# A list scheduler that plans PSUM tiles as exclusive and lets a tile pass one other in its ring

## The chip, the cores and the metric

The kernel runs on one core of one Trainium2 chip. Time is device microseconds of one execution, the median of 3 runs. The engines are TensorE (PE in the profile, with its weight loads as PEld), VectorE (DVE), ScalarE (ACT), GpSimd (POOL) and SyncE (SP), which here issues every DMA.

## The reference

Two layers of a sequence mixer over 2048 tokens of width 1024. Each layer normalises and modulates `x`, projects it once, runs two groups of four heads on the projection, joins them, projects back and adds the result to `x` with a gate.

```python
h = rms_norm(x, norm_g[l]) * (1.0 + scale[:, None]) + shift[:, None]
proj = h @ w_in[l]
gq, gk, gv, glr, gz, dq, dk, dv, dz = split_columns(proj)
...
o_gla = gla_branch(...)     # chunked linear attention: conv, forget gate, state scan, rms_norm, silu gate
o_diff = diff_branch(...)   # two softmax maps per head, p0 - lam * p1, chunk-causal; rms_norm, silu gate
y = jnp.concatenate([o_gla, o_diff], axis=-1).astype(x.dtype) @ w_out[l]
x = x + gate[:, None] * y
```

## The kernel before, in words

The 2048 tokens are cut into four units of 512. A dense product is made of three matmuls on 32-bit operands split in a high and a low half (`mm3`, `proj_T`): 128 by 128 weights against 512 columns, into one of the four PSUM tiles tagged `acc`. Each PSUM tile is 128 partitions by 512 values of 4 bytes. A second ring of four, tagged `tp`, holds the transposes (`tp`), the attention scores (`sc`) and the attention outputs (`po`).

Attention runs per layer, unit and head, 32 heads in all. `head_evac` reads a head's four `acc` tiles: per tile ScalarE copies q and k to `rw`, makes `th`, and copies v to `Vt`, and VectorE makes the gate `z` from `th` and the tile. In `qk_gen`, TensorE then transposes `rw` into two `tp` tiles. From the Q tile, ScalarE writes `qh` twice for each of two maps and VectorE writes `ql` (from the tile and `qh`) and copies it over to the other partitions; from the K tile, ScalarE writes half of `Kt` and VectorE the other half. `attn_gen` multiplies Q by K into `sc` tiles, which VectorE moves to `s` with a running minimum; ScalarE takes the exponential; TensorE transposes `s` (`tp<-ident,s`), ScalarE copies that to `aT`, and TensorE multiplies it by V into `po`.

The order of the work is not the order of that code. Python generators call a recorder (`Program.record`), which notes each instruction, the earlier ones it must follow, and the buffers it uses. `Program.order` then replays the record as a list scheduler with a table of costs and of latencies from engine to engine: it takes the engine that can start soonest, and the instruction of the lowest turn on it. `best_order` does that 60 more times with turns moved ahead of waits of TensorE, and keeps the order with the lowest planned end. `issue` emits that order; below it, a framework sets the semaphores that every instruction waits for, from the emitted order and the tiles touched.

Two rules of the planner matter here. An instruction follows earlier ones where one of the two writes what the other touches; for a PSUM tile any access is to the whole of it, but two readers are not ordered. And the tiles of one tag are given slots strictly in the order of the record (`nxt`): a tile whose predecessor has no slot yet must wait, even if a slot is free.

Of the kernel before, what the change touches and what calls it, by code (L numbers as in the profile page):

```python
# [35 lines left out]
class Buf:  # L36
    def __init__(self, pool, shape, dt, tag, name, bufs):
        self.pool, self.shape, self.dt, self.tag, self.name, self.bufs = pool, tuple(shape), dt, tag, name, bufs
        self.psum = pool.psum
        self.tile = None  # L40
# [80 lines left out]
class Program:  # L121
# [6 lines left out]

    def __init__(self, **engines):
        self.ops = []  # L130
        self.hist = {}
        self.group = {}
        self.engines = engines
# [10 lines left out]
    def record(self, e, method, args, kw):  # L144
        i = len(self.ops)
        views = [v for v in list(args) + list(kw.values()) if isinstance(v, View)]
        out = kw["out"] if "out" in kw else args[0]
        deps = set()
        for v in views:
            wr = v is out or v is kw.get("accum_out")  # L150
            h = self.hist.setdefault(v.buf, [])
            keep = []
            for j, w2, box in h:
                hit = all(a < d and c < b for (a, b), (c, d) in zip(box, v.box))
                if hit and (wr or w2) and j != i:
                    deps.add(j)
                if not (wr and all(c <= a and b <= d for (a, b), (c, d) in zip(box, v.box))):
                    keep.append((j, w2, box))
            keep.append((i, wr, v.box))
            self.hist[v.buf] = keep  # L160
        self.ops.append((e, method, args, kw, deps, self.cost(e, method, args, kw, out), {v.buf: 0 for v in views}))

    def together(self, first):

# [46 lines left out]
    def best_order(self, rounds=60):  # L211


        ops, rnd = self.ops, random.Random(0)
        turn = [float(i) for i in range(len(ops))]
        made = self.order(turn)
        best = self.span
        for _ in range(rounds):
            res, begin, end, ready = made
            lines = {e: [i for i in res if ops[i][0] == e] for e in "TAV"}  # L220
            place = {i: k for q in lines.values() for k, i in enumerate(q)}
            waits = [(begin[i] - end[j], i) for j, i in zip(lines["T"], lines["T"][1:]) if begin[i] - end[j] > 150]
            turn2 = list(turn)
            for wait, i in waits:
                if rnd.random() >= wait / 1500 * rnd.random():
                    continue
                first = begin[i] - 15000
                for _ in range(12):
                    e = ops[i][0]
                    i = max(ops[i][4], key=lambda j: end[j] + self.LAT[ops[j][0]][e], default=None)  # L230
                    if i is None or end[i] < first:
                        break
                    if (ops[i][0] in "AV" or ops[i][0] == "T" and i not in self.group) and begin[i] - ready[i] > 80:
                        q, k = lines[ops[i][0]], place[i] - 1
                        while k >= 0 and begin[q[k]] >= ready[i]:
                            turn2[i] = min(turn2[i], turn[q[k]] - 0.5)
                            k -= 1
            made2 = self.order(turn2)
            if self.span <= best:
                best, made, turn = self.span, made2, turn2  # L240
        self.span = best
        return made[0]

    def order(self, turn_of):
        ops, N = self.ops, len(self.ops)
        begin, finish = [0.0] * N, [0.0] * N
        left, uses, turn = {}, [], {}
        for o in ops:
            for b in o[6]:
# [2 lines left out]
                    turn.setdefault((b.pool, b.tag), []).append(b)  # L252
                left[b] += 1
        place = {b: k for q in turn.values() for k, b in enumerate(q)}
        nxt = dict.fromkeys(turn, 0)
        slots = {t: [{} for _ in range(q[0].bufs or q[0].pool.bufs)] for t, q in turn.items()}
        blocked = {t: [] for t in turn}
        slot, used = {}, {}
# [5 lines left out]
        ready = [0.0] * N  # L264
        free = dict.fromkeys(self.engines, 0.0)
        dma = 0.0
        pend = {e: [] for e in free}
# [4 lines left out]
        res, burst, mode = [], 0, 0  # L272
        while len(res) < N:
            while todo:
                now, todo = sorted(todo), []
                for i in now:
                    e, bufs = ops[i][0], ops[i][6]
                    new = {}
                    for b in sorted((b for b in bufs if b not in slot), key=place.get):
                        t = (b.pool, b.tag)  # L280
                        if place[b] != nxt[t] + new.get(t, 0) or len(slots[t]) <= new.get(t, 0):
                            blocked[t].append(i)
                            break
                        new[t] = new.get(t, 0) + 1
                    else:
                        for b in sorted(bufs, key=place.get):
                            if b not in slot:
                                t = (b.pool, b.tag)
                                slot[b] = min(slots[t], key=lambda u: max(u.values(), default=0.0))
                                slots[t].remove(slot[b])  # L290
                                used[b] = {}
                                nxt[t] += 1
                                todo += blocked[t]
                                blocked[t] = []
                            for e2, x in slot[b].items():
                                ready[i] = max(ready[i], x + (self.LAT[e2][e] if e != e2 or e == "S" else 0))
                        heapq.heappush(pend[e], (ready[i], turn_of[i], i))
            t, e = min((free[e] if avail[e] else max(free[e], pend[e][0][0]), e)
                       for e in free if avail[e] or pend[e])
            while pend[e] and pend[e][0][0] <= t:  # L300
                heapq.heappush(avail[e], heapq.heappop(pend[e])[1:])
            rest = [x for x in avail[e] if self.group.get(x[1]) == burst] if e == "T" and burst else ()
            if rest:
                i = min(rest)[1]
                avail[e].remove(min(rest))
                heapq.heapify(avail[e])
            else:
                i = heapq.heappop(avail[e])[1]
            if e == "T":
                burst = self.group.get(i, 0)  # L310
            if e == "S":
                dma = end = max(dma, t + 1150, flight[-8] + 2000) + ops[i][5]
                free[e] = max(t + 475, dma - 8000)
                flight.append(end)
            elif e == "A" and self.table(ops[i]) not in (None, table):
                table = self.table(ops[i])
                free[e] = end = t + ops[i][5] + 1283
            elif e == "T":
                if self.mode(ops[i]) != mode:
                    mode = self.mode(ops[i])  # L320
                    t += 160 if mode else 190
                w = int(t / win)
                warm = work.get(w - 1, 0.0) > 0.5 * win
                free[e] = end = t + ops[i][5] * (1 if warm else 2)
                if ops[i][1] == "transpose" or ops[i][2][2].shape[-1] > 1:
                    for v in range(w, int(end / win) + 1):
                        work[v] = work.get(v, 0.0) + min(end, (v + 1) * win) - max(t, v * win)
            else:
                free[e] = end = t + ops[i][5]
            res.append(i)  # L330
            begin[i], finish[i] = t, end
            for j in succ[i]:
                ready[j] = max(ready[j], end + self.LAT[e][ops[j][0]])
                nd[j] -= 1
                if nd[j] == 0:
                    todo.append(j)
            for b in ops[i][6]:
                used[b][e] = max(used[b].get(e, 0.0), end)
                left[b] -= 1
                if left[b] == 0:  # L340
                    t_ = (b.pool, b.tag)
                    slots[t_].append(used[b])
                    todo += blocked[t_]
                    blocked[t_] = []
        self.span = max(free.values()) / 1e3
        return res, begin, finish, ready

    def issue(self):
        real = lambda v: v.real() if isinstance(v, View) else v
# [978 lines left out]
```

## Time and profile before

| | us |
|---|---|
| median of 3 runs (2516.93 to 2519.32) | 2519.05 |
| the profiled execution | 2520.62 |
| its span | 2518.9 |
| TensorE busy in it | 2465.0 |
| VectorE busy | 1736.4 |
| ScalarE busy | 1285.0 |

A matmul's end in the profile is modelled: a 128 by 512 matmul shows about 0.40 us, while the next one starts about 0.23 us after it. Busy times are unions, so TensorE counts as busy for the last 0.16 us or so in which the pipeline drains. Idle time of TensorE is therefore a little less than what it lost. All recorded instructions carry one line, L355 (`issue`), so groups are told apart by tile names.

### The profile page before, as it was taken

The page shows a single profiled execution, that of the slowest core. Times are in us where ns is not written, and L with a number is a line of the kernel's source. Part 1 is how long each engine was busy: PE and PEld are TensorE (multiplying, and loading weights), DVE is VectorE, ACT ScalarE, POOL GpSimd, SP SyncE. Part 2 cuts the span into 40 slices and gives each one's busy share as a digit, 9 for nine tenths or more (in the row PEclk, how much of TensorE's full clock was granted, in tenths as well). Part 3 has the DMA queues.
Part 4 walks back from the last instruction along what each step waited for, and adds up shares of the span by engine and source line. Part 5 has one row for each costly group of instructions (what it writes and reads, how often), then busy time and mean ns, then how long its engine had stood idle before and what let it go on. Part 6 is the DMA issues. An engine that isn't in the chain of part 4 may idle for free.

```text
span 2518.9 us, 40492 instructions
## 1 busy us (share of the span) xinstructions
PE 2465.0 (98%) x13923; PEld 2025.2 (80%) x13923; DVE 1736.4 (69%) x5313; ACT 1285.0 (51%) x2760; POOL 136.2 (5%) x424
## 2 busy tenths in 40 slices
PE   8999999999999999999999999999999999999999
PEld 5787777887888888888688777888788888888887
DVE  4879767772777737677874884667636777286874
ACT  5656534562445534455763563445614556154552
POOL 0001000000000000000000010000000000000000
PEclk9999999999999999999999999999999999999999
DMA  8667876456453555444357767454474443734343
GB/s 266 251 233 281 286 247 208 156 191 211 163 186 105 189 186 172 141 136 163 109 204 267 265 247 254 169 187 153 161 251 153 142 162 119 262 102 147 130 147 126
DMA packets 204685, 474.00 MB, mean 188 GB/s; under 512 B 20736, under 2 KB 82368, under 8 KB 204480
## 3 DMA queue, kind: packets, MB, share of 16 engines
q1 hardware_dynamic: 204480, 471.41, 54.5%
q8 instruction: 111, 1.82, 0.3%
q14 instruction: 94, 0.77, 0.1%
HBM read 360.19 MB, written 111.15 MB: 187 GB/s over the span
## 4 chain that ended last, share of the span: by engine, by line
PE 79%; DVE 11%; ACT 5%; DMA 3%; issue 2%; POOL 0%; SPq 0%; POOLq 0%; ACTq 0%; DVEq 0%
PE acc L355 51%; PE sc L355 12%; PE po L355 9%; PE tp L355 7%; DVE s L355 3%; ACT qh L355 2%; DVE t L355 1%; DVE ql L355 1%; ACT s L355 1%; DMA wr<-in_w_ada_dram 1%; DVE w L355 1%; ACT t L355 1%; DVE am L355 1%; DMA Kj<-kd 1%; DVE r L355 0%
## 5 line engine op out<-in xcount | busy, mean ns | idle before, releaser
L355 PE MATMUL acc<-w,hhi 128*128 128x512 f32 x2560 | 840.5, 402 | 2.9 <-ACT w L355 1.4
L355 PEld LDWEIGHTS acc<-w,hhi 128*128 128x128 f32 x2560 | 463.7, 189 | 92.3 <-issue 4.8
L355 PE MATMUL acc<-w,hlo 128*128 128x512 f32 x1280 | 504.9, 394 | 0.0
L355 ACT ACTIVATE s<-s,mx 128x512 f32<-128x512 f32 (+15 forms) x256 | 308.2, 1204 | 291.4 <-DVE s L355 290.1
L355 PE MATMUL acc<-hhi,w 128*128 128x512 f32 x1024 | 360.0, 400 | 0.0
L355 PE MATMUL acc<-w,oh 128*128 128x512 f32 x1024 | 332.5, 398 | 2.7 <-DVE t L355 1.1
L355 DVE TENSOR_SCALAR_CACHE_REDUCE s<-sc,mx 64x64 f32<-64x64 f32 (+5 forms) x640 | 307.9, 485 | 33.0 <-PE sc L355 14.3
L355 PEld LDWEIGHTS acc<-w,hlo 128*128 128x128 f32 x1280 | 240.8, 188 | 49.0 <-issue 0.6
L355 PEld LDWEIGHTS acc<-w,oh 128*128 128x128 f32 x1024 | 189.6, 188 | 41.3 <-DVE t L355 2.6
L355 PEld LDWEIGHTS acc<-hhi,w 128*128 128x128 f32 x1024 | 192.0, 188 | 36.7 <-DVE w L355 0.4
L355 ACT COPY aT<-tp 128x512 f32<-128x512 f32 (+2 forms) x320 | 163.0, 523 | 88.2 <-PE tp L355 85.4
L355 PE MATMUL po<-Vj,aT 128*128 128x128 f32 x1536 | 204.4, 277 | 0.7 <-ACT aT L355 0.5
L355 PE MATMUL acc<-w,ol 128*128 128x512 f32 x512 | 201.5, 397 | 0.0
L355 PE MATMUL acc<-hlo,w 128*128 128x512 f32 x512 | 201.0, 393 | 0.0
L355 DVE SCALAR_TENSOR_TENSOR s<-s,r 128x512 f32<-128x512 f32 (+3 forms) x320 | 197.8, 667 | 3.0
L355 PEld LDWEIGHTS po<-Vj,aT 128*128 128x128 f32 x1536 | 190.4, 192 | 10.5 <-ACT aT L355 4.7
L355 DVE TENSOR_SCALAR_CACHE_REDUCE s<-sc 128x512 f32<-128x512 f32 (+4 forms) x256 | 158.2, 621 | 38.7 <-PE sc L355 34.5
L355 PE MATMUL tp<-ident,s 128*128 128x128 f32 x1088 | 172.9, 275 | 11.8 <-DVE ql L355 4.2
L355 PEld LDWEIGHTS tp<-ident,s 128*128 128x128 f32 x1088 | 131.9, 141 | 49.5 <-issue 12.8
L355 ACT COPY rw<-acc 128x256 f32<-128x256 f32 x128 | 48.1, 376 | 239.6 <-PE acc L355 239.6
L355 PE MATMUL sc<-Kj,qh 128*128 128x512 f32 x384 | 158.5, 413 | 3.3 <-DVE s L355 1.4
L355 ACT ACTIVATE qh<-tp,G 64x512 fp32r<-64x512 f32 x128 | 87.6, 684 | 137.1 <-PE tp L355 115.0
(183 smaller groups left out, 3682.8 us busy)
## 6 DMA issues: line engine op xcount, KB each, us to landing
w<-wd SPq DMA_DIRECT2D x424, 512.0 KB, 4.2
wd<-w SPq DMA_DIRECT2D x144, 512.0 KB, 3.7
raw<-in_w_in_dram SPq DMA_DIRECT2D x120, 256.0 KB, 5.0
Kj<-kd SPq DMA_DIRECT2D x48, 512.0 KB, 5.8
wr<-in_w_ada_dram SPq DMA_DIRECT2D x128, 128.0 KB, 3.2
kd<-Kt SPq DMA_DIRECT2D x24, 512.0 KB, 4.0
Vj<-vd SPq DMA_DIRECT2D x48, 256.0 KB, 5.4
wr<-in_w_ada_dram SPq DMA_DIRECT2D x8, 1024.0 KB, 7.4
```

Source lines behind the costliest of these rows:

```text
L355: getattr(self.engines[e], method)(*[real(a) for a in args], **{k: real(v) for k, v in kw.items()})
```

## The change

Three edits in `Program`. First, each instruction notes the PSUM buffers that it touches (`banks`), and `order` keeps, for every such buffer, the last instruction of each engine on it: one that touches the buffer from another engine starts only when these have ended, readers too. An instruction that is held goes back to its engine's queue with a new ready time (inside a group kept together, it waits in place). Second, `best_order` follows such holds as it follows dependences when it looks for what made TensorE wait. Third, `nxt` becomes `left_out`, the list of tiles without a slot: the first of it may take a free slot, and the second may pass it if another slot stays free. No arithmetic, tile or DMA is added or removed.

```diff
@@ record
         self.ops.append((e, method, args, kw, deps, self.cost(e, method, args, kw, out), {v.buf: 0 for v in views}))
+        self.banks.append({v.buf: 0 for v in views if v.buf.psum})
@@ best_order
-                    i = max(ops[i][4], key=lambda j: end[j] + self.LAT[ops[j][0]][e], default=None)
+                    i = max(ops[i][4] | {held.get(i, i)} - {i}, key=lambda j: end[j] + self.LAT[ops[j][0]][e], default=None)
@@ order
-        nxt = dict.fromkeys(turn, 0)
+        left_out = {t: list(q) for t, q in turn.items()}
...
-                        if place[b] != nxt[t] + new.get(t, 0) or len(slots[t]) <= new.get(t, 0):
+                        ahead = left_out[t].index(b, 0, 2) if b in left_out[t][:2] else N
+                        if len(slots[t]) <= ahead or new.get(t, 0) and ahead != new[t]:
                             blocked[t].append(i)
                             break
...
-                                nxt[t] += 1
+                                left_out[t].remove(b)
...
+            prior = [j for b in self.banks[i] for e2, j in bank.setdefault(b, {}).items() if e2 != e]
+            if prior:
+                last = max(prior, key=lambda j: finish[j] + self.LAT[ops[j][0]][e])
+                hold = finish[last] + self.LAT[ops[last][0]][e]
+                if hold > t:
+                    held[i], ready[i] = last, hold
+                    if not rest:
+                        heapq.heappush(pend[e], (hold, turn_of[i], i))
+                        continue
+                    t = hold
+            for b in self.banks[i]:
+                bank[b][e] = i
```

What that moves is seen in the emitted order. The first place is ScalarE in layer 0, unit 2, fourth head, from the copy ahead of its Q tile to behind its K tile. Names in brackets are the semaphores that the instruction waits for, one for each engine and several for DMA queues. Before:

```order
L355 COPY aT<-tp 128x512 [waits PE_49,Activation_49]
L355 ACTIVATE qh<-tp,G_614 64x512 [waits PE_49]
L355 ACTIVATE qh<-tp,G_614 64x512
L355 ACTIVATE qh<-tp,G_614 64x512 [waits DVE_49]
L355 ACTIVATE qh<-tp,G_614 64x512
L355 CAST Kt<-tp 64x512 [waits DMAHW6_49,DMAHW0_49,PE_49]
L355 CAST Kt<-tp 64x512
```

and after, at the same head:

```order
L370 COPY aT<-tp 128x512 [waits PE_49,Activation_49]
L370 ACTIVATE qh<-tp,G_630 64x512 [waits PE_49]
L370 ACTIVATE qh<-tp,G_630 64x512 x3
L370 CAST Kt<-tp 64x512 [waits DMAHW3_49,DMAHW0_49,PE_49]
L370 CAST Kt<-tp 64x512
```

The wait for VectorE between the second and the third `qh` is gone. It stands in 27 of the 32 heads before and in one after.

The second place is TensorE in the same head, from the PV matmuls behind the transposes of `rw` (Q and K) to the next transposes of `s`, which need a free `tp` slot. The waits are left out here. Before:

```order
L355 MATMUL po<-Vj,aT 128x128 x4
L355 MATMUL acc<-w,hhi 128x512 x2
L355 MATMUL acc<-w,hlo 128x512
L355 MATMUL acc<-w,hhi 128x512 x2
L355 MATMUL acc<-w,hlo 128x512
L355 MATMUL acc<-w,hhi 128x512 x2
L355 MATMUL acc<-w,hlo 128x512
L355 MATMUL tp<-ident,s 128x128 x4
```

and after:

```order
L370 MATMUL acc<-w,hlo 128x512
L370 MATMUL acc<-w,hhi 128x512 x2
L370 MATMUL acc<-w,hlo 128x512
L370 MATMUL acc<-w,hhi 128x512 x2
L370 MATMUL acc<-w,hlo 128x512
L370 MATMUL acc<-w,hhi 128x512 x2
L370 MATMUL acc<-w,hlo 128x512
L370 MATMUL acc<-w,hhi 128x512 x2
L370 MATMUL acc<-w,hlo 128x512
L370 MATMUL acc<-w,hhi 128x512 x2
L370 MATMUL acc<-w,hlo 128x512
L370 MATMUL tp<-ident,s 128x128 x4
```

Nine dense matmuls stood between them, and sixteen do now.

The third place is TensorE in layer 1, unit 0, second head: from the transposes of K to the first scores that read `Kt`. Before:

```order
L355 MATMUL tp<-ident,rw 128x128 x4
L355 MATMUL acc<-w,oh 128x512 x2
L355 MATMUL acc<-w,ol 128x512
L355 MATMUL acc<-w,oh 128x512 x2
L355 MATMUL acc<-w,ol 128x512
L355 MATMUL acc<-w,oh 128x512 x2
L355 MATMUL acc<-w,ol 128x512
L355 MATMUL acc<-w,oh 128x512 x2
L355 MATMUL sc<-Kt,qh 128x128
```

and after, the rows just ahead of the same matmul:

```order
L370 MATMUL acc<-w,oh 128x512 x2
L370 MATMUL acc<-w,ol 128x512
L370 MATMUL acc<-w,oh 128x512 x2
L370 MATMUL acc<-w,ol 128x512
L370 MATMUL acc<-w,oh 128x512 x2
L370 MATMUL acc<-w,ol 128x512
L370 MATMUL acc<-w,oh 128x512 x2
L370 MATMUL acc<-w,ol 128x512
L370 MATMUL acc<-w,oh 128x512 x2
L370 MATMUL acc<-w,ol 128x512
L370 MATMUL acc<-w,oh 128x512
L370 MATMUL sc<-Kt,qh 128x128
```

Eleven dense matmuls stood between the transposes and the scores; now there are nineteen, so that the transposes are no longer among the twelve rows.

## Rows read from the trace of the kernel before

**Rows 1.** The page's part 1: busy time of each engine, share, instructions.

```profile
PE 2465.0 (98%) x13923; PEld 2025.2 (80%) x13923; DVE 1736.4 (69%) x5313; ACT 1285.0 (51%) x2760; POOL 136.2 (5%) x424
```

**Rows 2.** Busy times by stretch: the first 63 us.

```profile
core 0: us, PE busy (x) PEld busy (x) DVE busy (x) ACT busy (x) POOL busy (x), PEclk, DMA share, GB/s
0.00:63.00 63.00, 51.51 (x320) 33.27 (x320) 31.24 (x111) 34.24 (x70) 4.27 (x16) 1.00 0.87 266
```

**Rows 3.** Waits of PE: who for whom, us in total, times, longest.

```profile
PE sc L355 <- DVE Kt L355: 7.4, 11, 1.1
...
PE tp L355 <- DVE ql L355: 4.2, 4, 1.1
PE tp L355 <- DVE s L355: 4.0, 7, 1.5
PE tp L355 <- DVE z L355: 3.1, 6, 1.5
PE po L355 <- ACT aT L355: 2.6, 5, 1.0
PE sc L355 <- DVE s L355: 2.4, 6, 0.6
...
PE tp L355 <- ACT aT L355: 1.8, 2, 0.9
...
PE acc L355 <- DVE z L355: 0.4, 1, 0.4
```

**Rows 4.** Waits of DVE and ACT between accesses to one PSUM tile.

```profile
DVE z L355 <- ACT Vt L355: 116.7, 52, 18.4
...
DVE ql L355 <- ACT qh L355: 80.3, 50, 4.7
...
ACT qh L355 <- DVE ql L355: 21.2, 26, 1.6
```

**Rows 5.** Timeline, layer 0, unit 2, fourth head: start, length, engine, tiles, idle.

```profile
826.36 1.38 ACT L355 ACTIVATE qh<-tp,G 64x512 fp32r<-64x512 f32 x2 [0.59 <-PE tp L355]
...
827.77 0.74 DVE L355 SCALAR_TENSOR_TENSOR ql<-tp,G,qh 64x512 fp32r<-64x512 f32 x1 [1.64 <-PE po L355]
...
828.54 1.38 ACT L355 ACTIVATE qh<-tp,G 64x512 fp32r<-64x512 f32 x2 [0.81 <-DVE ql L355]
...
829.42 0.39 PE L355 MATMUL acc<-w,hlo 128*128 128x512 f32 x1
...
829.96 0.76 DVE L355 SCALAR_TENSOR_TENSOR ql<-tp,G,qh 64x512 fp32r<-64x512 f32 x1 [0.99 <-ACT qh L355]
...
830.86 0.63 PE L355 MATMUL tp<-ident,s 128*128 128x128 f32 x4 [1.05 <-DVE ql L355]
```

**Rows 6.** Timeline, layer 1, unit 0, second head.

```profile
1312.82 0.60 PE L355 MATMUL tp<-ident,rw 128*128 128x128 f32 x4
...
1313.96 0.62 PE L355 MATMUL acc<-w,oh 128*128 128x512 f32 x2
1314.42 0.39 PE L355 MATMUL acc<-w,ol 128*128 128x512 f32 x1
...
1315.33 0.61 PE L355 MATMUL acc<-w,oh 128*128 128x512 f32 x2
1315.59 0.42 DVE L355 CAST ql<-ql 64x512 fp32r<-64x512 f32 x1
1316.04 1.41 DVE L355 TENSOR_TENSOR Kt<-tp,Kt 64x512 fp32r<-64x512 f32 x2
1316.78 0.33 PE L355 MATMUL sc<-Kt,qh 128*128 128x128 f32 x1 [0.83 <-DVE Kt L355]
```

**Rows 7.** Groups by shape: the four readers of an `acc` tile in `head_evac`.

```profile
L355 ACT COPY rw<-acc 128x256 f32<-128x256 f32 x128 | 48.1, 376 | 239.6 <-PE acc L355 239.6
...
L355 ACT COPY Vt<-acc 128x128 f32<-128x128 f32 x128 | 35.9, 280 | 0.0
L355 ACT ACTIVATE th<-acc 128x128 f32<-128x128 f32 x128 | 35.8, 288 | 1.4 <-DVE z L355 1.1
...
L355 DVE SCALAR_TENSOR_TENSOR z<-th,acc 128x128 f32<-128x128 f32 x128 | 35.7, 284 | 118.4 <-ACT Vt L355 116.7 <-ACT th L355 1.1
```

**Rows 8.** Groups by shape: the commonest move of scores out of PSUM.

```profile
L355 DVE TENSOR_SCALAR_CACHE_REDUCE s<-sc,mx 128x512 f32<-128x512 f32 x192 | 143.6, 748 | 17.3 <-PE sc L355 12.4 <-PE tp L355 0.3
```

More of the change, by code (lines that the diff above doesn't have):

```diff
@@ L130, in __init__ @@
         self.ops = []
+        self.banks = []
         self.hist = {}
@@ L218, in best_order @@
         for _ in range(rounds):
-            res, begin, end, ready = made
+            res, begin, end, ready, held = made
             lines = {e: [i for i in res if ops[i][0] == e] for e in "TAV"}
@@ L245, in order @@
         ops, N = self.ops, len(self.ops)
-        begin, finish = [0.0] * N, [0.0] * N
+        begin, finish, held, bank = [0.0] * N, [0.0] * N, {}, {}
         left, uses, turn = {}, [], {}
@@ L345, in order @@
         self.span = max(free.values()) / 1e3
-        return res, begin, finish, ready
+        return res, begin, finish, ready, held
     def issue(self):
```

## The prediction

> **What bounds the kernel now.** I read the busy times first. TensorE is busy for 2465.0 of 2518.9 us, VectorE for 1736.4, ScalarE for 1285.0 [rows 1]. So the time is TensorE's, and a change of order can win only what TensorE stands idle: 2518.9 - 2465.0 = 53.9 us. Next the stretches: 63.00 - 51.51 = 11.5 us of that lies in the first 63 us, where the DMA engines are 0.87 busy with loads that no order makes shorter; the clock is granted in full there [rows 2]. That leaves 42.4 us. One correction raises the prize. Dense matmuls start (1314.42 - 1313.96) / 2 = 0.23 us apart but are shown 0.39 long [rows 6], so a wait behind one has cost 0.16 us more than its idle time says.
>
> Then I asked for TensorE's waits alone [rows 3]. The largest group is scores that wait for VectorE's half of `Kt`: 7.4 us in 11 waits. Next are transposes of `s` that wait for `ql`: 4.2 us in 4. They do not read `ql`; they need a `tp` slot, and `ql` is the last reader of the Q tile in it. Both hang on one piece of work, the emptying of the Q tile, so I read that in the timeline [rows 5]. ScalarE writes two `qh`, then idles 0.81 us for VectorE's `ql`; VectorE then idles 0.99 us for the next two `qh`; TensorE idles 1.05 us at the end. No data pass from that `ql` to the third `qh`: both only read the tile. The program thus already holds two readers of a PSUM tile apart, and the old planner, which does not order readers, did not know. Over the kernel `qh` waits 21.2 us for `ql`, `ql` 80.3 us for `qh` (part of this is data), and `z` 116.7 us for `Vt`, with no data between [rows 4]. The order of before was made for evacuations that end earlier than they do.
>
> [...]
>
> **The change part by part.** It issues the same instructions; costs come from where TensorE's instructions stand. I counted matmuls between producer and user in the emitted order of both.
>
> *Q tile.* From the first `qh` to the end of the last `ql` took 826.36 to 830.72, so 4.36 us [rows 5]. With four `qh` and then two `ql` it is 4 x 0.69 + 2 x 0.75 and a handover of 0.04, so 4.30: the emptying is hardly faster. What changes is that TensorE does other work meanwhile. Sixteen dense matmuls instead of nine stand there, 7 x 0.23 = 1.6 us more, of which up to 0.4 goes because transposes of `s` now stand among those of `rw`; the stall was 1.05 + 0.16 = 1.21. Besides, the transposes of `s` at all four such places now wait in the order for ScalarE alone or for nothing: their slot is one that an `aT` copy frees, and the Q tile's goes to a later tile. Gain 4.2 + 4 x 0.16 = 4.8 us.
>
> *K tile.* The halves of `Kt` on VectorE stand behind the copy of `ql` (0.42) and take 1.41 us [rows 6]. Before, the first map's copy ran while ScalarE made the second pair of `qh`; now both copies stand behind the second `ql`, so `Kt` is ready 0.42 - 0.06 = 0.36 us later. In the head shown there are 19 instead of 11 matmuls, 8 x 0.23 = 1.84 us more, against 0.83 + 0.16 + 0.36 = 1.35: the stall goes. In the other heads that stalled the order gives 0.9 to 3.6 us more, and in one 0.46, which leaves about 0.5 us. No head has less than 18 matmuls there now; before some had 9. The 11 waits cost 7.4 + 11 x 0.16 = 9.2 us, of which I take 8.7 as gained.
>
> *Copies to `aT`.* Two transposes wait 1.8 us together for a slot held by an `aT` copy [rows 3]. The order gives each two matmuls more: 2 x 0.46 = 0.9 us gained.
>
> *The other waits.* 42.4 - 7.4 - 4.2 - 1.8 = 29.0 us of idle time are left, in small groups such as the transposes of `s` and `z` [rows 3]. What is late there is VectorE or ScalarE with its queue. A planner that knows that `z` will stand waiting for `Vt` can put other work ahead; the 116.7 us [rows 4] are idle time of an engine that has 782 us of it, so little reaches TensorE. At the same places the order now has between two matmuls fewer and four more, more often more. Bounds: all of it gone, -29; or as much again through bad luck of a new order, +29. Nearest is the row of `tp<-DVE s`, where half a microsecond per wait is at stake and mostly one or two matmuls (0.23 to 0.46) were added at some. I take a tenth, -3.
>
> *New waits.* In `head_evac`, `z` now comes last behind `Vt` in nearly all tiles. Where a new dense group takes over the `acc` tile, the order leaves 7, 7, 9 and 13 matmuls at four places, while before the least was 14, where one wait of 0.4 us stood [rows 3]. The four readers need 0.376 + 0.288 + 0.280 + 0.284 = 1.23 us [rows 7] if ScalarE comes at once, and 7 matmuls are 1.6 us: lower bound 0. If they need what the place with 14 did, 14 x 0.23 + 0.56 = 3.8 us, the loss is 2.2 + 2.2 + 1.7 + 0.8 = 6.9: upper bound. I take a third, +2.4, as the shown durations fit into 1.6 us. Behind such a wait TensorE's whole queue stands, so it counts in full. DMAs keep their number; where loads of `raw`, `Kj` and `Vj` move past one another on SyncE, I cost it at nothing, because no wait of TensorE for data is among the large rows after the start.
>
> *Sum.* -4.8 - 8.7 - 0.9 - 3.0 + 2.4 = -15.0 us. The profiled execution took 2520.62 (its span 2518.9 and 1.7 around it), so it would be 2505.6; the median of the runs is 1.6 us lower, so 2504.
>
> **The rivals.** *The waits only move.* A planner's order is drawn anew, and most of the waits are not tied to a shared tile. If the 29.0 us of the others grow by half, 14.5, they eat the gain: 2518 to 2520. For it: the search accepts orders by planned ends, and what it planned was often wrong by half a microsecond. Against it: the order keeps its large shape; the work ahead of each head's scores is within a few microseconds of where it was, and at the places of the old waits the distance is more often longer.
>
> *Passing costs slots.* In the `tp` ring a score tile that passes a transposed tile takes one of four slots, so that the ring turns on three. TensorE then waits at a score matmul for VectorE to move older scores out, 0.748 us a piece [rows 8]. Today that is 2.4 us in 6 waits, or 0.4 + 0.16 = 0.56 each [rows 3], of 640 groups of scores. It decides from 27 more such waits on (27 x 0.56 = 15); 50 would give 28 - 15 = 13 us more than before, 2532. Against it: the matmuls between the move of a score tile and its slot's next user are in the order about as many as before.
>
> *The whole lag goes.* If VectorE and ScalarE now run as planned, half of the other 29 us goes instead of a tenth: 11.5 us more, about 2492. For it: the planner's one known error is mended. Against it: most of those waits hang on queues, not on shared tiles.
>
> *The plan is too cautious.* The second map's `qh` reads other partitions of the Q tile than the first map's `ql`. If the two could overlap, the plan would hold 0.75 us too much in each of 32 heads; TensorE's work that it moves there to fill it would be missing elsewhere, up to 24 us in all: 2504 + 24 = 2528. Against it: `qh` did wait for `ql`, 26 times [rows 4], and the wait stands in the program, which the change does not touch. [...]
>
> **How the numbers follow.** Forecast 0.62, within 2496 to 2512. The waits only move: 0.17. Passing costs slots: 0.08. The plan is too cautious: 0.02. The whole lag goes: 0.11. The predicted time is the forecast's, 2504. The range goes from 2490, which takes in most of the last case, to 2521, which takes in the case of no gain; the two slow cases are left out. A difference of 0.2%, 5 us, is about what a measurement can tell from no change: faster than 2514 has 0.62 + 0.11 and a little of the second case, 0.74; within 0.2% 0.16; slower 0.10.
>
> **What would show it right or wrong.** In the profile after, TensorE's waits for `Kt` should fall from 7.4 to under 1 us and those for `ql` from 4.2 to none; `qh` should no longer wait for `ql`; TensorE's busy time should stay near 2465 minus about 3 (the drained tails), and its idle time fall from 53.9 to about 41. If `sc<-DVE s` rises above 15 us, the slots decided it. If `Kt` and `ql` fall as said but the idle time stays, the waits moved. If `acc<-DVE z` comes to more than 5 us, I undercounted the four short places.

## The result: 0.8% faster, and the profile after

The changed kernel takes 2499.78 us (median of 4, 2496.81 to 2504.76) against 2519.19 for the one before: a ratio of 0.992, with a 95% interval of 0.9904 to 0.9935. The forecast was 2504, in a range of 2490 to 2521. The profiled execution took 2496.81 us with a span of 2495.0, against 2518.9. It is the fastest of the four, while the profiled one before was slower than its own four, so the spans differ by 23.9 us and the medians by 19.4. The granted clock is 0.999 of full speed in both profiled executions, so the gain is not one of the clock.

The page's part 1 after, the same columns as [rows 1]:

```profile
span 2495.0 us, 40505 instructions
...
PE 2455.7 (98%) x13923; PEld 2029.5 (81%) x13923; DVE 1736.7 (70%) x5313; ACT 1287.7 (52%) x2760; POOL 139.0 (6%) x424
```

VectorE and ScalarE work as long as before; TensorE's idle time is 2495.0 - 2455.7 = 39.3 us instead of 53.9. Its waits, who for whom, us in total, times, longest, as in [rows 3] (the view lists waits of more than 0.15 us):

```profile
PE tp L370 <- DMA wr<-in_w_ada_dram: 5.0, 2, 4.0
PE tp L370 <- DVE s L370: 4.7, 9, 2.1
PE tp L370 <- DVE z L370: 3.1, 5, 1.5
...
PE po L370 <- ACT aT L370: 2.1, 3, 1.2
...
PE acc L370 <- DVE z L370: 1.7, 3, 1.2
...
PE sc L370 <- DVE s L370: 1.0, 2, 0.6
...
PE tp L370 <- ACT aT L370: 0.7, 1, 0.7
```

What is not there matters most: no row `PE sc <- DVE Kt` (7.4 us before) and no row `PE tp <- DVE ql` (4.2). All rows of this view together fell from 47.4 us in 69 waits to 33.9 in 47. Waits of `tp` for `aT` fell from 1.8 to 0.7, and `acc<-z` rose from 0.4 to 1.7. Experiment 8 below ran the same order once more and shows how far such rows move by themselves: 36.2 us in 48 waits, idle time 41.2 us, `acc<-z` 0.8.

The stretch of [rows 2], the first 63 us, after:

```profile
0.00:63.00 63.00, 49.65 (x312) 32.65 (x314) 29.51 (x106) 33.01 (x66) 3.88 (x16) 1.00 0.90 270
```

Here TensorE stands idle for 13.35 us, 1.9 more than before (12.16, or 0.7 more, in experiment 8); all of the gain lies later.

The timeline of the head of [rows 6], after:

```profile
1296.69 2.77 ACT L370 ACTIVATE qh<-tp,G 64x512 fp32r<-64x512 f32 x4 [4.18 <-PE tp L370]
...
1298.31 0.60 PE L370 MATMUL tp<-ident,rw 128*128 128x128 f32 x4
...
1299.50 1.53 DVE L370 SCALAR_TENSOR_TENSOR ql<-tp,G,qh 64x512 fp32r<-64x512 f32 x2 [4.23 <-ACT qh L370]
...
1301.06 0.88 DVE L370 CAST ql<-ql 64x512 fp32r<-64x512 f32 x2
...
1301.97 1.41 DVE L370 TENSOR_TENSOR Kt<-tp,Kt 64x512 fp32r<-64x512 f32 x2
...
1303.08 0.22 PE L370 MATMUL sc<-Kt,qh 128*128 128x128 f32 x1
```

From the first `qh` to the end of the last `ql` are 1299.50 + 1.53 - 1296.69 = 4.34 us; 4.30 was forecast, and 4.36 had been before in the head of [rows 5]. Over all 32 heads the median of this time is 4.36 us before and 4.35 after. So the Q tile is emptied no faster, and `Kt` comes no earlier. But TensorE now reaches the scores 4.77 us after the first transposes of K (3.96 in [rows 6]), and their row names no idle time ahead of them: it has done dense work in between.

The waits between accesses to one tile are still there:

```profile
DVE z L370 <- ACT Vt L370: 124.8, 56, 17.9
...
DVE ql L370 <- ACT qh L370: 71.5, 21, 4.9
```

In [rows 4] they were 116.7 and 80.3 us. Only `qh` for `ql`, 21.2 us there, has no row any more. The planner did not remove the turns that engines take at a tile. It counts on them.

### The profile page after: what moved, and what is told of

It reads as the page before. It is cut to its first block, busy times and chain, and to the rows that moved or that the text cites. A ratio compares the mean times of both kernels' runs of the same rounds, so it can differ in the third digit from the quotient of the medians.

```text
span 2495.0 us, 40505 instructions
## 1 busy us (share of the span) xinstructions
PE 2455.7 (98%) x13923; PEld 2029.5 (81%) x13923; DVE 1736.7 (70%) x5313; ACT 1287.7 (52%) x2760; POOL 139.0 (6%) x424
## 4 chain that ended last, share of the span: by engine, by line
PE 80%; DVE 11%; DMA 4%; ACT 2%; issue 2%; POOL 0%; SPq 0%; POOLq 0%; DVEq 0%; ACTq 0%
PE acc L370 52%; PE sc L370 11%; PE po L370 9%; PE tp L370 8%; DVE s L370 4%; DMA wr<-in_w_ada_dram 2%; DVE t L370 1%; DMA w<-wd 1%; DVE w L370 1%; DVE am L370 1%; ACT t L370 1%; DVE ql L370 1%; ACT s L370 1%; DVE r L370 1%; DVE vN L370 0%
## 5 line engine op out<-in xcount | busy, mean ns | idle before, releaser
L370 DVE SCALAR_TENSOR_TENSOR s<-s,r 128x512 f32<-128x512 f32 (+2 forms) x320 | 197.7, 667 | 2.4
L370 PE MATMUL sc<-Kj,ql 128*128 128x512 f32 x384 | 151.5, 395 | 0.0
```

The costliest lines, as they stand in the source:

```text
L370: getattr(self.engines[e], method)(*[real(a) for a in args], **{k: real(v) for k, v in kw.items()})
```

## Experiments

All were timed beside the kernel before on the same chip; only ratios are compared between groups (1 to 4, 5 to 8, 9 to 12). The kernel before had medians of 2520.75 to 2521.17 there.

**1. Holds alone.** The slot rule is put back to recorded order.

```diff
-                        ahead = left_out[t].index(b, 0, 2) if b in left_out[t][:2] else N
-                        if len(slots[t]) <= ahead or new.get(t, 0) and ahead != new[t]:
+                        k = new.get(t, 0)
+                        if b not in left_out[t][k:k + 1] or len(slots[t]) <= k:
```

> The holds stay, tiles take slots strictly in recorded order again. Theory (the gain is TensorE work that the planner puts beside the emptying of the Q and K tiles, because it now knows that readers of one PSUM tile take turns): most of the 19 us stays, 2501 to 2508; TensorE's waits for Kt under 2 us, none for ql. Four heads have less than 18 dense matmuls ahead of their first scores on Kt in this order, so a little of the Kt waits may be back. Rival 1 (passing in the ring gives the gain): 2514 to 2520. Rival 2 (luck of a newly drawn order): no relation to the holds, anything from 2505 to 2530, with the Kt waits as before or not.

Measured: 2512.47 us, ratio 0.9967 (0.9956 to 0.9979), -8.6 us. The theory and rival 1 both miss it, and only the wide range of rival 2 takes it in; the `Kt` and `ql` waits went as the theory said. TensorE's waits, same columns:

```profile
PE tp L370 <- DVE oss L370: 3.1, 3, 1.5
...
PE acc L370 <- DMA w<-wd: 2.2, 4, 0.9
PE tp L370 <- DVE vN L370: 1.9, 2, 1.6
...
PE sc L370 <- DMA Kj<-kd: 1.4, 2, 0.9
...
PE sc L370 <- DVE Kt L370: 0.3, 1, 0.3
```

The two groups that the prediction was about are gone as it said (7.4 to 0.3, 4.2 to none). But all waits together are 44.0 us in 64, only 3.4 less than before: others have grown by 8 us, among them loaded weights (`w<-wd`, 0.3 before), `oss` (1.1) and `vN` (0.4).

**2. Passing alone.** No instruction notes a PSUM buffer, so nothing is held.

```diff
-        self.banks.append({v.buf: 0 for v in views if v.buf.psum})
+        self.banks.append({})
```

> Passing stays, the holds are left out. Theory: 2512 to 2521; 27 heads alternate qh and ql again and eleven have less than 18 matmuls ahead of Kt, so TensorE's waits for Kt are 5 us or more and those for ql 3 us or more. Rival 1 (passing): 2499 to 2505. Rival 2 (luck): anything.

Measured: 2520.11 us, ratio 0.9995 (0.9986 to 1.0003): no difference. The waits that the holds cure are back:

```profile
PE sc L370 <- DVE Kt L370: 6.6, 9, 0.9
...
PE tp L370 <- DVE ql L370: 2.5, 4, 1.0
```

The `ql` waits, 2.5 us, are under the 3 that was expected. So the holds are worth 8.6 us by themselves, passing nothing that can be told from no change, and both together 19. The gain is no sum of its parts.

**3. Holds for the Q tiles alone**, without passing.

```diff
-        self.banks.append({v.buf: 0 for v in views if v.buf.psum})
+        self.banks.append({v.buf: 0 for v in views if v.buf.psum and getattr(v.buf, "hold", False)})
...
             ps = tp()
+            ps.buf.hold = g == 0
```

> Holds for the Q tile of each head alone (32 of some 1500 PSUM tiles), no passing. Theory: the Kt and ql waits hang on this one tile, so 13 to 14 us of the gain are here: 2503 to 2509, Kt waits under 2.5 us, none for ql. Rival (the gain is the better plan of VectorE's and ScalarE's queues everywhere, the z behind Vt above all): 2513 to 2520.

Measured: 2515.14 us, ratio 0.9979 (0.9971 to 0.9988), -5.9 us. The time is in the rival's range and outside the theory's. The two waits went as expected, and their worth was not what was expected: `PE sc <- DVE Kt` is 1.2 us in 3 waits and `PE tp <- DVE ql` has no row, yet less than half of 13 us arrives at the end. Better queues everywhere, the rival's cause, are tried by themselves next.

**4. Holds for all tiles but Q**, without passing: the same edit with `not getattr(...)`.

> Holds for every PSUM tile except the Q tiles, no passing. Theory: 2512 to 2519, with Kt waits of 5 us or more (14 heads have less than 18 matmuls there) and ql waits of 3 us or more. Rival (better queues everywhere): 2501 to 2508.

Measured: 2518.63 us, ratio 0.9993 (0.9984 to 1.0002): no difference. `PE tp <- DVE ql` is back at 4.1 us in 4 waits; `PE sc <- DVE Kt` came to 3.7 in 9, under the 5 that was expected. So most of what the holds alone give hangs on the Q tile; the rest, 8.6 against 5.9 us, is within what two draws differ by (experiments 5 to 7). That the planner knows of `z` behind `Vt` is worth nothing that can be measured alone.

**5. Another seed, kernel before.** `random.Random(1)` in place of `random.Random(0)` in the search.

> The kernel before with another seed of its search (1 instead of 0): how much of a difference is the luck of one draw. Theory (holds and passing each mend a real error of the plan, and need one another): within 5 us of the kernel before, 2514 to 2526, Kt waits of 5 us or more and ql waits again. Rival (luck): a seed moves the time as much as the change did, 10 to 20 us either way.

Measured: 2524.54 us, ratio 1.0015 (1.0006 to 1.0024), +3.4 us, with `Kt` waits of 7.6 us in 11 and `ql` waits of 4.1 in 4: the same two groups in another draw.

**6. Another seed, holds alone.** The edits of 1 and 5 together.

> Holds without passing, seed 1. With seed 0 this took 0.33% off, 8.5 us, and the full change 19. Theory of interplay: again between the two, 2508 to 2517, no ql waits and Kt waits under 2 us. Rival (seed 0 was an unlucky draw, and the holds alone are worth the whole): 2498 to 2505.

Measured: 2516.48 us, ratio 0.9975 (0.9965 to 0.9985), -4.7 us; no `Kt` and no `ql` row. That is against the kernel before with seed 0. Against experiment 5, the kernel before with the same seed, it is 2524.54 - 2516.48 = 8.1 us, close to the 8.6 of seed 0. Holds alone are worth some 8 us, not 19.

**7. Another seed, full change.** The seed alone is edited.

> The full change, seed 1. Theory of interplay: 2496 to 2507, at least 6 us under holds alone with the same seed. Rival (seed 0 was a lucky draw of the full change): 2507 to 2516, like the holds alone.

Measured: 2505.97 us, ratio 0.9937 (0.9924 to 0.9949), -15.2 us, and 10.5 under experiment 6. Against experiment 5, with the same seed, it is 2524.54 - 2505.97 = 18.6 us. Seed 1 was slower than seed 0 in all three kernels, by some 3 to 7 us; with either seed the change is worth 18 us or more over the kernel before with that seed.

**8. The search does not follow holds.** The second edit is undone.

```diff
-                    i = max(ops[i][4] | {held.get(i, i)} - {i}, key=lambda j: end[j] + self.LAT[ops[j][0]][e], default=None)
+                    i = max(ops[i][4], key=lambda j: end[j] + self.LAT[ops[j][0]][e], default=None)
```

> The full change without its second edit: the search does not follow holds when it looks for what made TensorE wait. Theory: the holds act in the planner's replay, not in the search's choice of what to move, so the time stays within 4 us of the full change, 2497 to 2505, with no Kt or ql waits. Rival (the search must see the holds): 2508 or more.

Measured: 2498.72 us, ratio 0.9907 (0.9894 to 0.9921). The emitted order is the same as that of the full change on every engine, so this edit has no effect here, and the run is a second measurement of the change, -22.5 us. Its profiled execution (span 2498.0 us) has TensorE busy for 2456.8 us, and the row of `acc<-z` in it is

```profile
PE acc L370 <- DVE z L370: 0.8, 3, 0.3
```

against 1.7 in 3 for the same order above. Differences of that size between two profiles show nothing.

**9. Passing in the PSUM rings only, with all holds.**

```diff
-                        if len(slots[t]) <= ahead or new.get(t, 0) and ahead != new[t]:
+                        if len(slots[t]) <= ahead or (new.get(t, 0) or not t[0].psum) and ahead != new.get(t, 0):
```

> The holds for all PSUM tiles; passing only in the two PSUM rings, SBUF rings in recorded order. Holds alone took 8.5 us off, both together 19 to 22. Theory A (a held PSUM tile blocks the ring of tp, and passing there lets score tiles go ahead): most of the further gain, 2498 to 2504. Theory B (passing matters in SBUF rings, where weights, Kj, Vj and scratch tiles are loaded or written ahead): as holds alone, 2509 to 2516.

Measured: 2514.09 us, ratio 0.997 (0.9958 to 0.9981): as holds alone.

**10. Passing in the SBUF rings only, with all holds.** The same line with `t[0].psum` in place of `not t[0].psum`.

> The holds for all PSUM tiles; passing only in SBUF rings, PSUM rings in recorded order. Theory A: as holds alone, 2509 to 2516. Theory B: 2498 to 2504; no head has less than 18 dense matmuls ahead of its scores on Kt here, which speaks for B at that place.

Measured: 2504.22 us, ratio 0.9933 (0.9921 to 0.9946), -16.5 us: most of the whole, and 0.2 us above the range of theory B. So theory B holds for the time, with one seed. Of TensorE's waits, those for loaded keys, `PE sc <- DMA Kj<-kd`, are 1.0 us before, 1.4 with holds alone, 2.3 with the other seed, 0.7 with passing in PSUM, and have no row in any of the seven kernels in which SBUF tiles may pass, experiment 2 included. But these are 1 to 2 us, and experiment 2 lost them without a gain. All waits together are 43.2 us in 61 here, hardly less than the 44.0 in 64 with holds alone, although the time is 8 us shorter. The pages' part 1, of experiment 1 (span 2510.8) and of this one (span 2502.4):

```profile
PE 2461.4 (98%) x13923; PEld 2027.2 (81%) x13923; DVE 1737.5 (69%) x5313; ACT 1285.4 (51%) x2760; POOL 136.8 (5%) x424
...
PE 2454.1 (98%) x13923; PEld 2028.4 (81%) x13923; DVE 1734.7 (69%) x5313; ACT 1288.6 (51%) x2760; POOL 139.4 (6%) x424
```

The spans differ by 8.4 us: 7.3 of it is time in which TensorE is shown busy, with as many matmuls and a granted clock of 0.999 in both, and 1.1 is idle time. Counted from start to start in the two traces, the matmuls of 512 columns that are followed by no wait of over 0.15 us take 1896.8 us (7933 of them) with holds alone and 1889.6 (7930) here. So passing in SBUF does not pay by shorter waits in the view; what makes these intervals shorter is not known, and which ring does it was not tried.

**11. Two tiles may be passed.**

```diff
-                        ahead = left_out[t].index(b, 0, 2) if b in left_out[t][:2] else N
+                        ahead = left_out[t].index(b, 0, 3) if b in left_out[t][:3] else N
```

> The full change with two tiles that may be passed instead of one, each while slots stay free for them. If passing is worth what it frees: a little faster than the full change, 2494 to 2500. If one is enough and a wider choice only uses up slots: 2500 to 2508, with more TensorE waits for score tiles.

Measured: 2501.41 us, ratio 0.9923 (0.9909 to 0.9938): no gain over one. Its waits for moved scores, 2.4 us in 6, are more than the 1.0 in 2 of the change and no more than before.

**12. 150 rounds of the search** instead of 60.

> The full change with 150 instead of 60 rounds of the search. The plan can only become better by its own costs. If what is left of TensorE's waits is in the plan: 2492 to 2499. If it is in what the plan does not know (queues, loads): 2497 to 2505, no difference beyond the spread of seeds, about 6 us.

Measured: 2496.80 us, ratio 0.9904 (0.9891 to 0.9918). It is the lowest median, in the first range and just outside the second, but the interval overlaps those of the change and of experiment 8, so a gain over the change is not shown.

## Why the prediction was right, and where it was not

*What bounds.* Right. The time fell with TensorE's idle time, and with its busy time (below), while the other engines' busy times stayed (VectorE 1736.4 and 1736.7 us, ScalarE 1285.0 and 1287.7).

*Q tile.* Right in mechanism and size: the four waits for `ql` are gone, and the emptying took 4.34 us for a forecast of 4.30. *K tile.* Right: 7.4 us went to no row, where 0.5 was allowed to stay. Experiments 1, 3 and 6 show that the holds on the Q tile are what removes both; without them the `ql` waits stay (2.5 us in 2, 4.1 in 4) and most or half of the `Kt` waits (6.6 and 3.7).

*Copies to `aT`.* The wait fell by 1.1 us; 0.9 was forecast.

*The other waits.* Forecast -3.0 for these and +2.4 for new ones. Idle time after the first 63 us that belongs to none of the three named groups went from 29.0 to 25.2 us: 39.3 - 13.35 - 0.7 = 25.2. That is -3.8, new waits included; the same sum from experiment 8, the same order, is 41.2 - 12.16 - 0.7 = 28.3, so -0.7. Both agree with the forecast of -0.6 for the two terms together, no more closely than two profiles of one order agree. `acc<-z` rose by 1.3 us, or by 0.4 in experiment 8, so the +2.4 was too much; and a third of 6.9 is 2.3, not 2.4. The start-up, which I had taken as fixed, lost 0.7 to 1.9 us.

*The sum.* The median fell by 19.4 us, and by 22.5 in experiment 8; -15.0 was forecast. Idle time fell to 39.3 us, 41.2 in experiment 8, where about 41 was forecast. What was too small is the fall of TensorE's busy time. I charged 0.16 us of a draining matmul for each of 15 waits, 2.4 in all, and expected about 3. It fell by 9.3, and by 8.2 in experiment 8. Twenty-two fewer waits in the view make 3.5 of the 9.3, by the same estimate of 0.16 us each. The other 5.8 lie at matmuls that are followed by no wait of over 0.15 us; they may be stalls too short for the view, but that was not measured by itself.

*The cause was only half named.* The 14.4 us of the three terms for Q, K and `aT` all come from places where the holds act, and the sum takes for granted that a wait removed is time won. Experiment 1 removes 11.3 us of idle time at `Kt` and `ql`, or an estimated 13.5 with tails of 0.16 us, and wins 8.6, while other waits grow by 8; experiment 3 removes 10.4 of idle time and wins 5.9; experiment 6 wins 8.1 over its own seed. That the dense matmuls which now stand between K and its scores are missing at other places fits these numbers, but was not followed to those places. I had written down just that mechanism, under the plan that is too cautious, and priced it on a ground that was not tested (partitions) at 0.02. The other 10 us or so need passing beside the holds (7 against 6: 10.5 us), most of it in the SBUF rings (10 against 1: 8 us). The sum took passing at nothing. That it still came within 5 us is partly luck: it counted too much for the waits removed and left out what passing adds.

*The rivals.* "Passing costs slots" is wrong: waits for moved scores fell from 2.4 to 1.0 us, and passing in the PSUM rings alone neither helps nor hurts (9 against 1). "The waits only move" is refuted for the whole and partly true for the holds alone. "The whole lag goes" did not happen: 25 to 28 of 29 us are still there. Whether the second map's `qh` can overlap the first map's `ql`, on which "The plan is too cautious" turns, was not put to a test: no edit changes how the semaphores are set, and in the traces before and after none of the 64 `ql` that read a Q tile overlaps any of the 128 `qh`. In the 0.81 us of [rows 5] ScalarE was about to read partitions 64 to 127 while VectorE read 0 to 63 (`qk_gen`): that wait shows that the program's semaphores go by the whole tile.

*What stays open.* Why the holds without passing make other waits grow by 8 us is not known. Passing in SBUF rings alone does not cure it: waits other than `Kt` and `ql` are 35.8 us before, 43.7 with holds alone, 43.2 with holds and passing in SBUF, and 33.9 after the full change (35.5 in experiment 8, 39.9 with seed 1). By which way passing in SBUF shortens TensorE's busy time is open too. Another seed moved a result by 3 to 7 us, so differences of that size between single variants, such as 1 against 3, are not settled, and the 8 us of 10 against 1, taken with one seed, is not far above it.

## What to carry to other kernels

If a planner or a person orders work by hand, read in the trace which waits have no data behind them, such as two engines that read one PSUM tile (here `qh` behind `ql`, 21.2 us, and `z` behind `Vt`, 116.7 us [rows 4]), and put them into the plan; the turns stayed here (`z` behind `Vt` came to 124.8 us after), but other work could be put beside them. A removed wait need not pay in full: here other waits took back a part. Look for rules that pin the order for another reason, here the strict order of tiles in a ring, and try loosening both together. Try another seed of any random search before the two parts of a change are compared, and compare kernels of one seed: here a seed moved the time by 3 to 7 us of 2500. And run one order twice before a small row of a profile is explained.

## What the runs showed of the hardware

Nothing that goes against what was expected. One thing was larger than expected: TensorE's busy time as the profile counts it fell by 9.3 us (8.2 in experiment 8) with the same 13923 matmuls, while its idle time fell by 14.6 (12.7). About 3.5 us of it is, by estimate, the tails of 22 waits: a dense matmul is shown about 0.16 us longer than the 0.23 us after which the next one started [rows 6]. The rest is not explained. So behind a busy share of 98% there was more time to win, over half as much as in the idle time.
